# A gated DeltaNet stage: decay rows loaded a pair ahead, convolutions without cleared columns, block merges ordered behind a value's transposes

## The chip, the cores and the metric

One core of a Trainium2 chip runs the whole program in one launch. The metric is the device time of that launch in microseconds (us), the median of several runs. Three runs of the kernel before took 2161.83, 2160.51 and 2162.01 us, median 2161.83.

The core has TensorE (PE; its weight loads are PEld), VectorE (DVE), ScalarE (ACT), GpSimd (POOL) and SyncE (SP). Here every DMA is issued from SP, in one queue and in order. Each engine works through its own list in order as well: an instruction that waits holds up all that stand behind it on that engine.

## The reference, cut to what matters

Two layers of a decoder on 512 prompt tokens and 8 sample tokens, model width 1024: a gated DeltaNet mixer, an MLP, a dilated sliding-window attention, an MLP. The change touches the DeltaNet alone:

```python
proj = x @ w_in                                  # q | k | v | z | b | a
qkv, new_buf = causal_conv_silu(qkv, conv_buf, conv_w)   # 4 taps along time, zeros before the prompt's start
q, k = l2norm(q) * dk ** -0.5, l2norm(k)         # 8 heads, shared by 16 value heads
beta, g = sigmoid(b), -exp(a_log) * softplus(a + dt_bias)
gc = cumsum(g)                                   # within a chunk
decay = where(causal, exp(gc[i] - gc[j]), 0)
a_strict = where(strict, (beta * k) @ k.T * decay, 0)
t_inv = inverse(eye + a_strict)                  # unit lower triangular
u, w = t_inv @ (beta * v), t_inv @ (beta * k * exp(gc))
# a scan over chunks with state S (128 x 128 per head):
v_new = u - w @ S
o = (q * exp(gc)) @ S + (q @ k.T * decay) @ v_new
S = S * exp(gc_last) + (k * exp(gc_last - gc)).T @ v_new
y = (rmsnorm(o) * silu(z)) @ w_out
```

The outputs also hold the last three rows before the convolution (prompt_state_conv, sample_state_conv).

## The kernel before, in words

All four stages keep x transposed on chip, model width on the partitions and 520 tokens (512 prompt, 8 sample) in the free dimension. A product with a weight (`Common.proj`, L156) runs as three float32r passes (L164 to L166: high by high, high by low, low by high) over 8 blocks of 128 rows, in two halves of 260 columns: 48 matmuls for 128 output features. Weights come from memory by SP (L145), ACT rounds them to a high part (L130) and DVE subtracts for the low part (L131).

The DeltaNet stage (`gdn`, L367) goes over 8 pairs of value heads; a pair shares a q/k head, and a chunk is 128 tokens, so a pair has 4 chunks by 2 heads = 8 units. Of a pair p:

- `key` and `query` (L542, L561) and `values` (L681) project 128 features each through `project` (L509). It clears 3 columns of a row tile `pre` on POOL (L512), copies the projection behind them (L516, L518, on ACT), copies the 8 sample columns to `news` (L519) and the prompt's last three columns to `tail` (L522, on POOL), and runs the four taps: one on ACT (L524), three on DVE (L526), which read `pre` at shifts 2, 1, 0; then tanh into a third row tile (L528) and the product with it (L530). Eight row tiles go round.
- `decay` (L584) loads gc of each token, as a row, to all 128 partitions (L591, 512 KB, from the DRAM tile `Dg`), straight into the tile `ET` (two buffers). DVE subtracts the column (L592), ACT takes the absolute value and exp (L593, L594), and DVE multiplies with the dot products of the keys (L607) to `E` (L599).
- `invert` (L618) sends the 32 x 32 diagonal blocks of E through DRAM (L625, L628) to POOL, which inverts them by 62 multiply and add instructions in a row (L634, L637), and sends them back (L638, L642) into `Uf`, a part of `held`.
- `attend` (L610) turns ET into the masked attention (L614, L615).
- `merge` (L645) builds the 128 x 128 inverses from the 32 x 32 blocks: three DVE transposes (L649 to L651) and small matmuls (L656, L664, L667, L673, L678) with ACT copies between.
- `values` also transposes its two convolved rows on PE (L690) into PSUM and scales them on DVE (L691).
- `scan` (L694) runs the four chunks: L705, L708, L711, L713, L716, L720, L727, L731. The last reader of ET is L727 of the last chunk.
- `sample` (L792) updates the sample's states: matmuls (L812), small DVE operations (L813 to L819), a transpose on PE (L822), a sum on PE (L838). `out` (L843) normalises and gates (L855, L858, transposes L863 on PE, L865 on DVE); `out_proj` multiplies with the output weights (L888 adds to x).

What sets the order: the program is written in the order of L898 to L932, and a planner at build time orders each engine's list, by its own estimate of when operands are ready and by priority. `decay`, `invert`, `merge`, `scan`, `sample` and `out` are `urgent` (L33): priority 2000 places ahead of their place in the text, so before projections that are written far above them. Tiles of one tag are handed out in the order of the text; the PSUM tag `pre` has two banks, for L577, L607, L690 and L863 alike, so the bank of pair p's L690 comes free when DVE has read L863 of pair p-1 (L865). Merge of pair 0 (L903) stands ahead of the loop, that of a later pair at L915.

Of the kernel before, what the change touches and what calls it, by code (L numbers as in the profile page):

```python
# [10 lines left out]
F32 = mybir.dt.float32  # L11
# [8 lines left out]
P = 128  # L20
# [346 lines left out]
def gdn(K, l, done):  # L367
# [8 lines left out]
    with ExitStack() as ctx:  # L376
# [6 lines left out]
        sizes = dict(Uf0=U * P, Uf1=U * P, T64=U * 64, hist=32 * 3 * NS, news=32 * NS, eyeU=8 * 32, convw=32 * CONV, tri=P, Uo0=8 * 32, Uo1=8 * 32, tail=32 * 3, beg=160, gcl=128, egc=192, sbc=256, id8=8, onorm=1, alog=16, dtb=16, bat=160)  # L383
# [3 lines left out]
        Ufs, T64, hist, news = [part("Uf0", P), part("Uf1", P)], part("T64", 64)[:64], part("hist", 3 * NS), part("news", NS)  # L387
        eyeU, convw, tri, tail = part("eyeU", 32), part("convw", CONV), part("tri", P)[:, 0], part("tail", 3)
# [117 lines left out]
        def row(name):  # L506
            return K.tile(gp, [P, T], F32, tag="row", name=name, bufs=8)

        def project(w, ft, dest=None):  # L509

            pre = row("pre")
            nc.gpsimd.memset(pre[:, 0:3], 0.0)  # L512

            def ev(ps, hf, s):
                if hf == 0:
                    nc.scalar.copy(pre[:, 3 : 3 + H], ps)  # L516
                else:
                    nc.scalar.copy(pre[:, 3 + H : 3 + NP], ps[:, : H - NS])  # L518
                    nc.scalar.copy(news[:, ft, :], ps[:, H - NS :])  # L519

            K.proj(w, mov, ev)
            nc.gpsimd.tensor_copy(tail[:, ft, :], pre[:, NP : NP + 3])  # L522
            a = row("conv")[:, :NP]
            nc.scalar.activation(a, pre[:, 3 : 3 + NP], AF.Copy, scale=convw[:, ft, 3:4])  # L524
            for j in (2, 1, 0):
                nc.vector.scalar_tensor_tensor(a, pre[:, j : j + NP], convw[:, ft, j : j + 1], a, ALU.mult, ALU.add)  # L526
            t = row("tanh")[:, :NP]
            nc.scalar.activation(t, a, AF.Tanh)  # L528
            dest = a if dest is None else dest
            nc.vector.scalar_tensor_tensor(dest, t, 1.0, a, ALU.add, ALU.mult)  # L530
            return dest

        class Pair:
# [48 lines left out]

            @urgent
            def decay(self):  # L584


                p, hh, kq, col = self.p, self.hh, self.kq, self.col
                E = self.E = K.tile(gp, [P, U, P], F32, tag="E", name="E", bufs=2)
                ET = self.ET = K.tile(gp, [P, U, P], F32, tag="ET", name="ET", bufs=2)
                E4 = ET.rearrange("p (c v) d -> p c v d", v=2)  # L590
                nc.sync.dma_start(E4, Dg[None, :, hh, :].to_broadcast([P, C4, 2, P]))  # L591
                nc.vector.tensor_tensor(E4, E4, gc[:, :, hh, None].to_broadcast([P, C4, 2, P]), ALU.subtract)  # L592
                nc.scalar.activation(ET, ET, AF.Abs)  # L593
# [164 lines left out]
            def sample_conv(self, i0, n, f0):  # L758
# [4 lines left out]
                nc.vector.tensor_tensor(a[:, d], news[:, fs], wj(3), ALU.mult)  # L763
# [140 lines left out]
        for p in range(QK_HEADS):  # L904
# [29 lines left out]
        nc.sync.dma_start(O["sample_state_conv"][l, :, 0:2, :], sc[:, 1:3, :])  # L934
        for i in range(2):
            ps = K.bank("cb")
            nc.tensor.transpose(ps[:, :P], news[:, 16 * i : 16 * i + 16, :].rearrange("p f b -> p (f b)"), ident)
# [5 lines left out]
        nc.tensor.transpose(ps[:96, :P], tail.rearrange("p f j -> p (f j)"), ident)  # L943
# [448 lines left out]
```

## Time and profile before

| what | us |
|---|---|
| median of three runs | 2161.83 |
| the profiled execution, its own time | 2166.66 |
| its span, first to last instruction | 2164.9 |
| PE busy in the span | 1992.7 (92%) |
| DVE busy | 1312.6 (61%) |
| ACT busy | 893.7 (41%) |
| POOL busy | 519.7 (24%) |

The profiled execution is 4.83 us above the median, and 1.8 us of its time lie outside the span. The DeltaNet stage takes about the first 790 us; the first MLP follows to about 1215 us, then the attention and the second MLP. Busy PE is an upper bound of its work, since matmuls overlap; the granted clock says at how much of 2.4 GHz TensorE ran.

### The profile page before, as it was taken

What the parts mean: (1) busy time and instruction counts of PE and PEld (TensorE: products, weight loads), DVE (VectorE), ACT (ScalarE), POOL (GpSimd) and SP (SyncE); (2) the same over time, 40 slices, a digit from 0 to 9 for tenths busy, and PEclk for the clock granted to TensorE, in tenths of its full rate; (3) what the DMA queues carried; (4) which work ended last, traced back from release to release, by engine and by line L of the source; (5) the groups of instructions that cost most, each with busy time, mean ns of one, the idle gap of its engine ahead of it and who ended that gap; (6) DMA issues with size and microseconds to landing.
All of it is one profiled execution on the core that took longest, in us unless ns stands there. A gap on an engine that the chain in (4) does not pass through costs nothing.

```text
span 2164.9 us, 41794 instructions
## 1 busy us (share of the span) xinstructions
PE 1992.7 (92%) x16436; PEld 1958.9 (90%) x16436; DVE 1312.6 (61%) x3299; ACT 893.7 (41%) x2391; POOL 519.7 (24%) x813
## 2 busy tenths in 40 slices
PE   8768887977987989999999999999999989999998
PEld 7768877977877879999999999999999989999998
DVE  4745866757675585454455557676766785544444
ACT  4434444444344353323244545555555434233231
POOL 1262254535244230000001123332332250000000
PEclk8879889999889789999999999999999999999999
DMA  5324454765654538676766775544445342333332
GB/s 141 82 57 132 148 156 126 216 177 166 188 159 136 176 112 301 232 249 228 252 228 207 245 226 131 140 114 116 130 123 145 98 112 79 91 96 89 97 89 79
DMA packets 416278, 328.56 MB, mean 152 GB/s; under 512 B 48408, under 2 KB 404568, under 8 KB 413896
## 3 DMA queue, kind: packets, MB, share of 16 engines
q1 hardware_dynamic: 416080, 325.88, 50.0%
q8 instruction: 129, 2.11, 0.4%
q14 instruction: 69, 0.57, 0.1%
HBM read 302.19 MB, written 132.83 MB: 201 GB/s over the span
## 4 chain that ended last, share of the span: by engine, by line
PE 63%; DMA 11%; DVE 10%; POOL 9%; issue 4%; ACT 3%; SPq 1%; POOLq 0%; DVEq 0%; ACTq 0%
PE mm L164 18%; PE mm L166 18%; PE mm L165 18%; DMA Ft<-D 4%; POOL held L637 3%; POOL fs L634 3%; DMA ET<-Dg 2%; DMA X<-base 1%; DVE wlo L131 1%; DMA D<-held 1%; PE po L1199 1%; PE tr L1052 1%; DVE conv L526 1%; PE sco L1119 1%; DMA base<-X 1%
## 5 line engine op out<-in xcount | busy, mean ns | idle before, releaser
L164 PE MATMUL mm<-split,whi 128*128 128x260 f32 (+1 forms) x2960 | 866.9, 293 | 3.5 <-DVE base L781 2.3
L166 PE MATMUL mm<-split,wlo 128*128 128x260 f32 (+1 forms) x2960 | 854.7, 289 | 7.9 <-DVE wlo L131 7.9
L165 PE MATMUL mm<-split,whi 128*128 128x260 f32 (+1 forms) x2960 | 850.2, 287 | 0.5 <-DVE split L178 0.5
L166 PEld LDWEIGHTS mm<-split,wlo 128*128 128x128 f32 (+1 forms) x2960 | 567.5, 192 | 10.2 <-DVE wlo L131 9.2
L164 PEld LDWEIGHTS mm<-split,whi 128*128 128x128 f32 (+1 forms) x2960 | 568.6, 192 | 6.8 <-issue 2.7
L165 PEld LDWEIGHTS mm<-split,whi 128*128 128x128 f32 (+1 forms) x2960 | 568.2, 192 | 1.4 <-DVE split L178 0.7
L130 ACT CAST whi<-raw 128x1024 fp32r<-128x1024 f32 (+1 forms) x273 | 285.5, 1046 | 436.4 <-PE mm L165 414.8
L131 DVE TENSOR_TENSOR wlo<-raw,whi 128x1024 fp32r<-128x1024 f32 (+1 forms) x273 | 339.6, 1244 | 195.7 <-ACT whi L130 186.4
L166 PE MATMUL mm<-hh,wlo 128*128 128x260 f32 x1024 | 288.7, 282 | 0.0
L165 PE MATMUL mm<-hl,whi 128*128 128x260 f32 x1024 | 288.6, 282 | 0.0
L164 PE MATMUL mm<-hh,whi 128*128 128x260 f32 x1024 | 288.3, 283 | 0.0
L165 PEld LDWEIGHTS mm<-hl,whi 128*128 128x128 f32 x1024 | 193.1, 189 | 0.0
L166 PEld LDWEIGHTS mm<-hh,wlo 128*128 128x128 f32 x1024 | 192.8, 188 | 0.0
L164 PEld LDWEIGHTS mm<-hh,whi 128*128 128x128 f32 x1024 | 192.2, 188 | 0.0
L346 DVE TENSOR_TENSOR t<-mm,bc 128x260 f32<-128x260 f32 x128 | 54.8, 428 | 152.9 <-PE mm L166 152.9
L190 POOL TENSOR_TENSOR acc<-acc,sq 128x260 f32<-128x260 f32 x42 | 37.6, 906 | 386.3 <-ACT sq L189 385.9
L634 POOL TENSOR_TENSOR fs<-Ft,held 128x60 f32<-128x60 f32 (+24 forms) x248 | 93.0, 375 | 95.0 <-DMA Ft<-D 77.2
L130 ACT CAST hh<-q 128x260 fp32r<-128x260 f32 x128 | 52.4, 410 | 121.1 <-DVE q L333 121.1
L637 POOL TENSOR_TENSOR held<-held,fs 128x60 f32<-128x60 f32 (+24 forms) x248 | 95.6, 386 | 18.7
L526 DVE SCALAR_TENSOR_TENSOR conv<-pre,held,conv 128x512 f32<-128x512 f32 x96 | 78.7, 820 | 29.4 <-POOL pre L512 29.0
L164 PE MATMUL mm<-onh,whi 128*128 128x260 f32 x256 | 88.7, 350 | 7.2 <-DVE base L888 6.1
L131 DVE TENSOR_TENSOR hl<-q,hh 128x260 fp32r<-128x260 f32 x128 | 54.8, 428 | 57.0 <-ACT hh L130 57.0
(379 smaller groups left out, 3270.3 us busy)
## 6 DMA issues: line engine op xcount, KB each, us to landing
out_dram<-in_cache_kv_w_dram SPq DMA_DIRECT2D x112, 832.0 KB
raw<-in_dsw_w_in_dram SPq DMA_DIRECT2D x72, 512.0 KB
raw<-in_mlp_w_up_dram SPq DMA_DIRECT2D x64, 512.0 KB
raw<-in_mlp_w_down_dram SPq DMA_DIRECT2D x64, 512.0 KB
raw<-in_gdn_w_in_dram SPq DMA_DIRECT2D x48, 512.0 KB
S<-in_state_gdn_dram SPq DMA_DIRECT2D x16, 512.0 KB
raw<-in_gdn_w_out_dram SPq DMA_DIRECT2D x16, 512.0 KB
ub<-Du SPq DMA_DIRECT2D x16, 512.0 KB
```

What stands on the lines that cost most here:

```text
L130: nc.scalar.copy(hi, src)
L131: nc.vector.tensor_tensor(lo, src, hi.bitcast(F32), ALU.subtract)
L164: nc.tensor.matmul(ps[:m], lhsT=w[0][:, k, :m], rhs=xh[:, s], start=k == 0, stop=False)
L165: nc.tensor.matmul(ps[:m], lhsT=w[0][:, k, :m], rhs=xl[:, s], start=False, stop=False)
L166: nc.tensor.matmul(ps[:m], lhsT=w[1][:, k, :m], rhs=xh[:, s], start=False, stop=k == nk - 1)
L190: nc.gpsimd.tensor_tensor(acc[:, s], acc[:, s], t, ALU.add)
L346: nc.vector.tensor_tensor(t, ps, r2[:, s], ALU.mult)
L526: nc.vector.scalar_tensor_tensor(a, pre[:, j : j + NP], convw[:, ft, j : j + 1], a, ALU.mult, ALU.add)
L634: nc.gpsimd.tensor_tensor(tmp[:, :m, :n], Ft[:, None, j + 1 :, j].to_broadcast([P, m, n]), Uo[:, :m, j : j + 1].to_broadcast([P, m, n]), A ...
L637: nc.gpsimd.tensor_tensor(Uo[:, :m, j + 1 :], Uo[:, :m, j + 1 :], tmp[:, :m, :n], ALU.add)
L1052: nc.tensor.transpose(pst[:, c], f[:, c * P : (c + 1) * P], ident)
L1119: nc.tensor.matmul(o, lhsT=qf[:, c * P : (c + 1) * P], rhs=kf[:, k0 * P : (c + 1) * P], start=True, stop=True)
```

## The change

Three parts, all in `gdn`:

1. `load_rows` is split from `decay`. It loads the rows of gc into a tile `rows` of its own (one buffer). Pair 0's rows are loaded ahead of its key, pair 1's behind pair 0's `decay`, and pair p+2's, with priority 2000, right behind `decay` of pair p+1. `decay` reads `rows` and writes ET.
2. `project` no longer clears columns. `pre` starts at column 0; tap j covers only the columns for which it has an input (511, 510 and 509 columns). Both halves are copied by one line; the last 11 columns (3 of the prompt, 8 of the sample) go to `news` in one copy, and the copy to `tail` on POOL is gone. Tanh goes into `pre`, so a projection needs two row tiles instead of three. At the end of the stage two DVE copies split `news` into two flat tiles, which the last transposes read.
3. `merge` of pairs 1 to 7 is traced under `issue_after` of two instructions: its DVE instructions are queued behind L530 of the pair's first value, and its PE instructions behind the last of the four L690 transposes of that value. This is an order of issue on the engine, with no semaphore of its own.

```diff
-sizes = dict(... news=32 * NS, ... tail=32 * 3, ...)
+sizes = dict(... news=32 * (3 + NS), ...)
 def project(w, ft, dest=None):
     pre = row("pre")
-    nc.gpsimd.memset(pre[:, 0:3], 0.0)
     def ev(ps, hf, s):
-        if hf == 0:
-            nc.scalar.copy(pre[:, 3 : 3 + H], ps)
-        else:
-            nc.scalar.copy(pre[:, 3 + H : 3 + NP], ps[:, : H - NS])
-            nc.scalar.copy(news[:, ft, :], ps[:, H - NS :])
+        nc.scalar.copy(pre[:, s], ps)
+        if hf:
+            nc.scalar.copy(news[:, ft], ps[:, H - NS - 3 :])
     K.proj(w, mov, ev)
-    nc.gpsimd.tensor_copy(tail[:, ft, :], pre[:, NP : NP + 3])
     a = row("conv")[:, :NP]
-    nc.scalar.activation(a, pre[:, 3 : 3 + NP], AF.Copy, scale=convw[:, ft, 3:4])
+    nc.scalar.activation(a, pre[:, :NP], AF.Copy, scale=convw[:, ft, 3:4])
     for j in (2, 1, 0):
-        nc.vector.scalar_tensor_tensor(a, pre[:, j : j + NP], convw[:, ft, j : j + 1], a, ALU.mult, ALU.add)
-    t = row("tanh")[:, :NP]
+        n = NP - 3 + j
+        nc.vector.scalar_tensor_tensor(a[:, NP - n :], pre[:, :n], convw[:, ft, j : j + 1], a[:, NP - n :], ALU.mult, ALU.add)
+    t = pre[:, :NP]
     nc.scalar.activation(t, a, AF.Tanh)
     dest = a if dest is None else dest
-    nc.vector.scalar_tensor_tensor(dest, t, 1.0, a, ALU.add, ALU.mult)
+    convs[0] = nc.vector.scalar_tensor_tensor(dest, t, 1.0, a, ALU.add, ALU.mult).ins
+def load_rows(self):
+    self.rows = K.tile(gp, [P, C4, 2, P], F32, tag="rows", name="rows", bufs=1)
+    nc.sync.dma_start(self.rows, Dg[None, :, self.hh, :].to_broadcast([P, C4, 2, P]))
 def decay(self):
-    nc.sync.dma_start(E4, Dg[None, :, hh, :].to_broadcast([P, C4, 2, P]))
-    nc.vector.tensor_tensor(E4, E4, gc[:, :, hh, None].to_broadcast([P, C4, 2, P]), ALU.subtract)
+    rows = self.rows
+    nc.vector.tensor_tensor(E4, rows, gc[:, :, hh, None].to_broadcast([P, C4, 2, P]), ALU.subtract)
 def values(self):
     for v in range(2):
         vf = project(wv[v], self.fts[2 + v])
+        if v == 0:
+            self.conv0 = convs[0]
...
         for c in range(C4):
-            nc.tensor.transpose(pst[:, c], vf[:, c * P : (c + 1) * P], ident)
+            flip = nc.tensor.transpose(pst[:, c], vf[:, c * P : (c + 1) * P], ident)
+        if v == 0:
+            self.flip0 = flip.ins
+pairs[0].load_rows()
 pairs[0].key()
 pairs[0].decay()
+pairs[1].load_rows()
...
     if p < last:
         pairs[p + 1].key()
         pairs[p + 1].decay()
+        if p + 1 < last:
+            with tc.high_priority(2000):
+                pairs[p + 2].load_rows()
...
     if p:
-        A.merge()
+        with tc.issue_after(A.conv0), tc.issue_after(A.flip0):
+            A.merge()
...
+flat = K.tile(gp, [P, 32 * (3 + NS)], F32, tag="flat", name="flat", bufs=1)
+tail, fresh = flat[:, : 32 * 3], flat[:, 32 * 3 :]
+nc.vector.tensor_copy(tail.rearrange("p (f j) -> p f j", j=3), news[:, :, :3])
+nc.vector.tensor_copy(fresh.rearrange("p (f b) -> p f b", b=NS), news[:, :, 3:])
```

## Rows read from the trace of the kernel before

**Rows 1.** The profile's page: the chain that ended last, its shares by engine.
```profile
PE 63%; DMA 11%; DVE 10%; POOL 9%; issue 4%; ACT 3%; SPq 1%; POOLq 0%; DVEq 0%; ACTq 0%
```

**Rows 2.** Stretches: engines' busy time (instructions), granted clock, DMA share, GB/s.
```profile
core 0: us, PE busy (x) PEld busy (x) DVE busy (x) ACT busy (x) POOL busy (x), PEclk, DMA share, GB/s
200.00:400.00 200.00, 169.70 (x1454) 163.18 (x1453) 135.98 (x417) 89.08 (x270) 77.57 (x155) 0.89 0.53 155
...
800.00:1200.00 400.00, 400.00 (x3321) 399.23 (x3321) 200.61 (x368) 138.99 (x276) 14.04 (x24) 1.00 0.70 240
```

**Rows 3.** Waits of PE, 0 to 800 us: waited for, us in total, times, longest.
```profile
PE sut L822 <- DVE base L815: 35.4, 6, 11.1
PE px L656 <- DMA held<-D: 16.2, 3, 6.0
PE son L838 <- DVE base L836: 9.1, 1, 9.1
PE sst L778 <- DVE base L766: 7.5, 1, 7.5
```

**Rows 4.** Waits of DVE, 0 to 800 us.
```profile
DVE held L649 <- DMA held<-D: 50.0, 6, 21.1
DVE ET L592 <- DMA ET<-Dg: 43.8, 8, 7.9
DVE conv L526 <- POOL pre L512: 29.0, 9, 6.6
```

**Rows 5.** Timelines of SP, DVE and PE at pair 2's rows: start, length, engine, line.
```profile
207.76 0.37 SPq L591 DMA_DIRECT2D ET<-Dg  x1
...
217.84 1.23 DVE L592 TENSOR_TENSOR ET<-ET,held 128x1024 f32<-128x1024 f32 x1 [7.43 <-DMA ET<-Dg]
...
219.59 0.28 PE L822 MATMUL sut<-base 128*16 128x128 f32 x1 [4.01 <-DVE base L815]
```

**Rows 6.** Timelines of DVE and PE where the same wait meets a merge.
```profile
451.30 0.43 DVE L649 STREAM_TRANSPOSE held<-held 32x256 f32<-32x256 f32 x1 [5.92 <-DMA held<-D]
...
451.92 0.37 PE L822 MATMUL sut<-base 128*16 128x128 f32 x1 [11.14 <-DVE base L815]
```

**Rows 7.** Stretches of PE before and behind that wait (columns as above).
```profile
437.80:440.80 3.00, 2.98 (x24) 2.77 (x24) 0.00 (x0) 0.27 (x1) 2.33 (x11) 1.00 0.80 84
452.00:455.50 3.50, 3.50 (x18) 3.50 (x17) 2.78 (x10) 0.26 (x1) 0.00 (x0) 0.50 1.22 405
```

**Rows 8.** Timeline of DVE at the second of the first two decays.
```profile
83.36 1.23 DVE L592 TENSOR_TENSOR ET<-ET,held 128x1024 f32<-128x1024 f32 x1 [3.42 <-DMA ET<-Dg]
```

**Rows 9.** Timelines of DVE and PE: a convolution's tap and the scan behind it.
```profile
592.86 0.88 DVE L526 SCALAR_TENSOR_TENSOR conv<-pre,held,conv 128x512 f32<-128x512 f32 x1 [6.56 <-POOL pre L512]
...
594.49 1.22 PE L705 MATMUL pk<-S,kq 128*128 128x256 f32 x2 [4.32 <-DVE S L720]
```

**Rows 10.** Timelines of PE and DVE: merge and first transposes of pairs 1, 2, 7.
```profile
224.82 0.56 PE L656 MATMUL px<-held,E 32*32 32x32 f32 x12
...
236.12 0.69 PE L690 MATMUL vtr<-base,conv 128*128 128x128 f32 x2
...
302.54 1.72 PE L656 MATMUL px<-held,E 32*32 32x32 f32 x32 [5.75 <-DMA held<-D]
...
305.78 0.74 DVE L865 SCALAR_TENSOR_TENSOR ot<-otr,held,sz 128x512 f32<-128x512 f32 x1
...
310.10 0.44 PE L690 MATMUL vtr<-base,conv 128*128 128x128 f32 x2
...
707.97 0.42 PE L656 MATMUL px<-held,E 32*32 32x32 f32 x4
...
724.40 0.38 PE L690 MATMUL vtr<-base,conv 128*128 128x128 f32 x2
```

**Rows 11.** Stretches of two POOL inversions, pair 1's and pair 2's (columns as above).
```profile
141.00:176.20 35.20, 34.82 (x331) 34.02 (x332) 26.27 (x74) 16.39 (x39) 30.89 (x69) 0.89 0.23 71
267.80:294.70 26.90, 23.24 (x184) 23.00 (x183) 11.67 (x39) 13.24 (x36) 22.15 (x61) 0.94 0.38 123
```

More of the change, by code (lines that the diff above doesn't have):

```diff
@@ L380, in gdn @@
         gp = setup.enter_context(tc.tile_pool(name="gset", bufs=1))
-        sizes = dict(Uf0=U * P, Uf1=U * P, T64=U * 64, hist=32 * 3 * NS, news=32 * NS, eyeU=8 * 32, convw=32 * CONV, tri=P, Uo0=8 * 32, Uo1=8 * 32, tail=32 * 3, beg=160, gcl=128, egc=192, sbc=256, id8=8, onorm=1, alog=16, dtb=16, bat=160)
+        sizes = dict(Uf0=U * P, Uf1=U * P, T64=U * 64, hist=32 * 3 * NS, news=32 * (3 + NS), eyeU=8 * 32, convw=32 * CONV, tri=P, Uo0=8 * 32, Uo1=8 * 32, beg=160, gcl=128, egc=192, sbc=256, id8=8, onorm=1, alog=16, dtb=16, bat=160)
         held = cp.tile([P, sum(sizes.values())], F32, name="held")
@@ L386, in gdn @@
         part = lambda n, d: held[:, at[n] : at[n] + sizes[n]].rearrange("p (a d) -> p a d", d=d)
-        Ufs, T64, hist, news = [part("Uf0", P), part("Uf1", P)], part("T64", 64)[:64], part("hist", 3 * NS), part("news", NS)
-        eyeU, convw, tri, tail = part("eyeU", 32), part("convw", CONV), part("tri", P)[:, 0], part("tail", 3)
+        Ufs, T64, hist, news = [part("Uf0", P), part("Uf1", P)], part("T64", 64)[:64], part("hist", 3 * NS), part("news", 3 + NS)
+        eyeU, convw, tri = part("eyeU", 32), part("convw", CONV), part("tri", P)[:, 0]
         beg = part("beg", 16).rearrange("p (c t) h -> p c t h", t=2)
@@ L507, in row @@
             return K.tile(gp, [P, T], F32, tag="row", name=name, bufs=8)
+        convs = [None]
         def project(w, ft, dest=None):
             pre = row("pre")
-            nc.gpsimd.memset(pre[:, 0:3], 0.0)
             def ev(ps, hf, s):
-                if hf == 0:
-                    nc.scalar.copy(pre[:, 3 : 3 + H], ps)
-                else:
-                    nc.scalar.copy(pre[:, 3 + H : 3 + NP], ps[:, : H - NS])
-                    nc.scalar.copy(news[:, ft, :], ps[:, H - NS :])
+                nc.scalar.copy(pre[:, s], ps)
+                if hf:
+                    nc.scalar.copy(news[:, ft], ps[:, H - NS - 3 :])
             K.proj(w, mov, ev)
-            nc.gpsimd.tensor_copy(tail[:, ft, :], pre[:, NP : NP + 3])
             a = row("conv")[:, :NP]
-            nc.scalar.activation(a, pre[:, 3 : 3 + NP], AF.Copy, scale=convw[:, ft, 3:4])
+            nc.scalar.activation(a, pre[:, :NP], AF.Copy, scale=convw[:, ft, 3:4])
             for j in (2, 1, 0):
-                nc.vector.scalar_tensor_tensor(a, pre[:, j : j + NP], convw[:, ft, j : j + 1], a, ALU.mult, ALU.add)
-            t = row("tanh")[:, :NP]
+                n = NP - 3 + j
+                nc.vector.scalar_tensor_tensor(a[:, NP - n :], pre[:, :n], convw[:, ft, j : j + 1], a[:, NP - n :], ALU.mult, ALU.add)
+            t = pre[:, :NP]
             nc.scalar.activation(t, a, AF.Tanh)
             dest = a if dest is None else dest
-            nc.vector.scalar_tensor_tensor(dest, t, 1.0, a, ALU.add, ALU.mult)
+            convs[0] = nc.vector.scalar_tensor_tensor(dest, t, 1.0, a, ALU.add, ALU.mult).ins
             return dest
@@ L762, in sample_conv @@
                 wj = lambda j: convw[:, fs, j : j + 1].to_broadcast([P, n, NS])
-                nc.vector.tensor_tensor(a[:, d], news[:, fs], wj(3), ALU.mult)
+                nc.vector.tensor_tensor(a[:, d], news[:, fs, 3:], wj(3), ALU.mult)
                 for j in range(3):
@@ L934, in gdn @@
         nc.sync.dma_start(O["sample_state_conv"][l, :, 0:2, :], sc[:, 1:3, :])
+        flat = K.tile(gp, [P, 32 * (3 + NS)], F32, tag="flat", name="flat", bufs=1)
+        tail, fresh = flat[:, : 32 * 3], flat[:, 32 * 3 :]
+        nc.vector.tensor_copy(tail.rearrange("p (f j) -> p f j", j=3), news[:, :, :3])
+        nc.vector.tensor_copy(fresh.rearrange("p (f b) -> p f b", b=NS), news[:, :, 3:])
         for i in range(2):
             ps = K.bank("cb")
-            nc.tensor.transpose(ps[:, :P], news[:, 16 * i : 16 * i + 16, :].rearrange("p f b -> p (f b)"), ident)
+            nc.tensor.transpose(ps[:, :P], fresh[:, P * i : P * (i + 1)], ident)
             r = K.tile(gp, [P, P], F32, tag="junk", name="cb", bufs=2)
@@ L942, in gdn @@
         ps = K.bank("cb")
-        nc.tensor.transpose(ps[:96, :P], tail.rearrange("p f j -> p (f j)"), ident)
+        nc.tensor.transpose(ps[:96, :P], tail, ident)
         r = K.tile(gp, [P, P], F32, tag="junk", name="cbt", bufs=2)
```

## The prediction

> **What bounds the kernel now.** I read the chain that ended last first: PE has 63% of it, DMA, DVE and POOL 30% together [rows 1]. The stretches say where those 30% sit. From 800 us on PE is never idle and its granted clock is 1.00; from 200 to 400 us, inside the DeltaNet stage, it is busy 169.70 of 200 us at 0.89 [rows 2]. So the rest of the kernel is bound by TensorE and the change does not touch it; the stage of the change, some 790 us long, is bound by what PE waits for. The table of PE's waits names it [rows 3], and that of DVE says why [rows 4]. 35.4 us go to L822, the transpose of the sample's update, which waits for a tiny DVE operation (L815). That operation is late because DVE stands still: in 43.8 us it waits at L592 for decay's rows, in 50.0 at the first of merge's transposes (L649), in 29.0 at a convolution's tap for a cleared column. DVE is an in-order list, so one wait for a DMA becomes everybody's.
>
> One case in full [rows 5]: SP issues pair 2's rows at 207.76, as soon as the scan two pairs back has released the ET buffer; L592 starts at 217.84, 10.1 us later, and DVE was idle for 7.43 of them; only then come L813 to L815, and PE, which had run out of other work in its list, starts L822 at 219.59 after 4.01 us idle.
>
> **Part 1, the rows a pair ahead.** A separate tile takes the load out of the release of ET. The same eight loads of 512 KB are issued, one each, so DMA traffic is unchanged. On SP's list a load now waits for L592 of the pair before instead of L727, and is issued about a pair earlier; the engines' mean DMA share there is 0.53 [rows 2], so it has room, and a landing late by several us is covered by the rest of the pair. L592 still waits for ET's release by L727, which is an engine's wait and no DMA's. The 43.8 us of DVE are the upper bound for DVE; what counts is PE's 35.4 in six waits. Of these some have a second cause: in the one of 11.14 us DVE stood at L649 from 445.4 to 451.30, 5.92 us, with L815 behind it [rows 6]. That is merge's wait and stays. I let 9 us stay in all (this 5.92, and half as much again for another of the kind) and take 26; the bounds are 17 and 35.4.
>
> At the start it may cost. Today the first two loads fly together and the second L592 runs at 83.36 after 3.42 us of waiting [rows 8]. With one buffer of rows, pair 1's load is issued only behind pair 0's L592, at about 79.9 (83.36 less 3.42); with the 10.1 us above it lands at 90.0, 6.6 later than now. If that L592 stays ahead of pair 0's E in DVE's list, the first inversion is 6.6 later and nothing covers it; if E goes first, the 7.5 us of L778 [rows 3] go as well. Bounds: a loss of 6.6, a gain of 7.5; I take a loss of 2, nearer to the row of the second L592.
>
> **Part 2, no cleared columns.** 32 clears and 32 small copies leave POOL; what they cost is not their length but their place, behind POOL's chain of 62 inversion steps. DVE's taps waited 29.0 us in nine cases [rows 4]. In the longest, 6.56 us, the scan's state update stood behind the tap and PE lost 4.32 at L705 [rows 9]: two thirds. Two thirds of all would be 19; zero is the other bound, for a tap that holds up nobody. I take 12, since only some of the nine fall into a scan. The shortened taps and the wider copies to `pre` and `news` keep their shapes to within a few columns: no difference. Two row tiles per projection instead of three let projections run further ahead; they already do, so nothing. The two added DVE copies at the stage's end have 96 and 256 columns and are shorter than L592's 1.23 us with 1,024 [rows 5]: 0.6 us, bounds 0 and 2.5, with out_proj of the last pair as cover.
>
> **Part 3, merge behind the first value's transposes.** DVE's half of the order changes nothing: the convolution it names is done long before. PE's half does. PE waits 16.2 us at L656 for the inverted blocks in three pairs [rows 3]; if four transposes and other matmuls go ahead of it, at most 16.2 is gained. Against it: L690 needs a PSUM bank that DVE frees by L865, after the pair before has been transposed out. In pair 2 L656 starts at 302.54 and L865 ends at 306.52, because it stands behind merge's own L649 on DVE; so PE may wait at L690 instead, and merge comes 4 us later [rows 10]. Behind the delayed merge stand the scan, then ET's release. How far merge could slip is read from how far the transposes follow it now: 11.3, 7.6 and 16.4 us in pairs 1, 2 and 7 [rows 10], mean 11.8, over seven pairs 82. I take 10 gained at L656 and 12 lost by later scans, a loss of 2: most of the slip should be absorbed, because the sample and output chain of the pair before, which now goes first, no longer shares PE and DVE with merge. Bounds: a gain of 16, a loss of 41 (half of 82).
>
> **The clock.** Ahead of the 11.14 us wait 24 matmuls take 3.0 us at granted clock 1.00 (2.4 GHz); behind it 18 take 3.5 at 0.50 (1.2 GHz) [rows 7]. At the first rate those 18 would take 2.25, so a long idle stretch costs 1.25 us more after it ends. Some five such stretches fewer give 6; bounds 0 and 10.
>
> **Sum.** 26 - 2 + 12 - 0.6 - 2 + 6 = 39.4 us. The profiled execution took 2166.66, 4.83 above the median of 2161.83; 2166.66 - 39.4 - 4.83 = 2122.4. I predict 2122.
>
> **The rivals.**
>
> *Merge comes too late* (slower). The place is the PSUM tag `pre`: merge of pair p now stands in line behind out of pair p-1, where today both run side by side, and the scan follows in series. The price is the 82 us above. Everything else gains 41.4; if half of the 82 reaches the end the change is worth nothing, if two thirds do (55), the kernel takes 2161.8 + 13.6 = 2175. For it: the distances, and that the last scan has little work of others beside it. Against: PE has projections to fill with. Chance 0.12.
>
> *The inversion's chain takes it all back.* E, the trip to POOL, 62 steps and the trip back are one chain per pair; if it is the true bound, what L822 gives up reappears at L656. POOL's steps depend on how busy DVE is: pair 1's inversion took 35.2 us with DVE busy 26.27 (75%), pair 2's 26.9 with DVE busy 11.67 (43%) [rows 11]. That is 8.3 us for 31 points. A DVE that no longer waits is busier during inversions: 10 points more would be 2.7 us each, 21 in eight pairs. Then the 26 of part 1 are gone and 3 of the clock's 6: 10.4 us remain, 2151. Against it: DVE's total work is the same, so what is done sooner is missing later. Chance 0.22.
>
> The Trainium skill, GPSIMD Engine Reference, Specifications, says that GpSimd shares its SBUF interfaces with VectorE and that DVE instructions with two SBUF inputs contend with it. By that rule L592, the taps and the low parts of weights, all with two such inputs, would slow the inversion; the two rows agree with it in sign.
>
> *More goes than I counted.* All upper bounds together (35.4 + 7.5 + 19 + 16 + 10 = 88) would give 2074; halfway from my sum, 2098. For it: a period that shrinks lets the next release come earlier as well. Against: L649's 50.0 us on DVE stay. Chance 0.16.
>
> *No effect*: the planner orders every list anew, and DVE's next wait, L649, takes the place of L592. 2162, chance 0.06.
>
> My forecast has 0.44; its own range is 2108 to 2140.
>
> **How the numbers follow.** Forecast, chain and more-than-counted are all faster: 0.44 + 0.22 + 0.16 = 0.82. Within 0.2% (4.3 us, about what a measurement of this kernel can tell from no change) 0.06, slower 0.12. The range reaches from 2088, which leaves out the lower third of the third rival, to 2160, which takes in the chain's 2151 and leaves out the slower case and no effect.
>
> **What would show it.** Right: the wait of DVE at L592 falls from 43.8 to under 8; L822's from 35.4 to about 9; no wait of L526 for POOL; the stretch 200 to 400 busier than 169.70 and its clock above 0.89. Part 3 right: L656 below 16.2 without a new wait of the same size at L690 or L711. Wrong: PE idle at L656 or L690 by as much as L822 lost; merges starting 8 us or more later against the pair's E; inversions of 30 us and over; the first E later than now by 5 us or more.

## The result, and the profile after

The changed kernel takes 2149.88 us (median of 4 runs, 2149.18 to 2152.49), the kernel before beside it 2161.92: a ratio of 0.9933, interval 0.9910 to 0.9957. That is 12 us, where 39.4 were forecast. The profiled execution took 2152.49 us, with a span of 2150.7 against 2164.9, so the traces hold 14.2 us of difference. (Here and below the ratios and intervals are the recorded ones; they differ a little from quotients of the medians, which would give 0.9944 here.)

The page's first part, span and busy time:

```profile
span 2150.7 us, 41729 instructions
PE 1972.8 (92%) x16436; PEld 1937.4 (90%) x16436; DVE 1319.7 (61%) x3301; ACT 892.5 (41%) x2391; POOL 500.4 (23%) x749
```

Read this first, against 1992.7 us of PE in 2164.9 before: the same 16,436 matmuls take 19.9 us less, and PE's idle time, span less busy, goes **up**, from 172.2 to 177.9. Whatever the change won, it did not win it by letting PE wait less. Line numbers have moved: L592 is now L596, L649 to L651 are L653 to L655, L656 is L660, L690 is L696, L822 is L830, L863 is L871.

The stretches, columns as in [rows 2]:

```profile
core 0: us, PE busy (x) PEld busy (x) DVE busy (x) ACT busy (x) POOL busy (x), PEclk, DMA share, GB/s
0.00:200.00 200.00, 160.20 (x1300) 155.36 (x1301) 114.99 (x335) 82.34 (x206) 68.21 (x161) 0.88 0.44 111
200.00:400.00 200.00, 159.77 (x1409) 153.17 (x1408) 138.59 (x409) 86.19 (x266) 74.26 (x141) 0.87 0.55 149
400.00:600.00 200.00, 173.71 (x1516) 168.53 (x1516) 152.62 (x442) 91.28 (x271) 86.51 (x175) 0.94 0.63 187
600.00:800.00 200.00, 156.18 (x1256) 147.75 (x1256) 124.53 (x349) 79.68 (x226) 67.74 (x115) 0.84 0.47 144
800.00:1200.00 400.00, 400.00 (x3323) 399.60 (x3323) 201.08 (x368) 139.58 (x288) 14.03 (x24) 1.00 0.70 242
```

From 200 to 400 us PE is busy less than in [rows 2] (159.77 against 169.70) and at a lower clock. From 800 to 1200 us nothing has changed. Now the waits of PE and of DVE up to 830 us:

```profile
PE px L660 <- DMA held<-D: 24.8, 1, 24.8
PE otr L871 <- DVE osb L866: 22.6, 3, 12.4
PE sut L830 <- DVE base L823: 18.0, 1, 18.0
PE mm L164 <- DVE base L848: 17.4, 1, 17.4
PE mm L166 <- DVE wlo L131: 13.1, 4, 11.4
PE son L846 <- DVE base L844: 11.6, 1, 11.6
PE mm L164 <- DVE ET L618: 6.3, 2, 4.1
```

```profile
DVE held L653 <- DMA held<-D: 91.0, 7, 19.6
...
DVE held L654 <- DMA held<-D: 26.7, 1, 26.7
...
DVE ET L596 <- DMA rows<-Dg: 7.8, 2, 4.1
```

The waits that the change aims at are gone: L596 for rows 7.8 us (43.8 in [rows 4], and both that remain lie at the start), no tap waits for POOL (29.0). But the first of merge's transposes wait 117.7 us (91.0 + 26.7), where before they waited 65.7 (50.0, and 15.7 at L650):

```profile
DVE held L650 <- DMA held<-D: 15.7, 3, 9.1
```

DVE got 65 us back and stands 52 us longer at its next DMA. PE has fewer and longer waits: one for 18.0 us at L830 instead of six for 35.4 [rows 3]. For pair 0's blocks it waits 24.8 us at L660; before it was

```profile
PE px L656 <- POOL fs L634: 15.7, 1, 15.7
```

One of the longer waits of the changed kernel, DVE and then PE:

```profile
268.45 0.22 DVE L844 TENSOR_TENSOR base<-base 128x16 f32<-128x16 f32 x1
288.24 0.43 DVE L653 STREAM_TRANSPOSE held<-held 32x256 f32<-32x256 f32 x1 [19.57 <-DMA held<-D]
...
289.67 0.17 DVE L848 TENSOR_SCALAR base<-son 128x16 f32<-128x16 f32 x1
```

```profile
272.16 0.30 PE L786 MATMUL sst<-base 128*128 128x24 f32 x2
289.90 0.59 PE L164 MATMUL mm<-split,whi 128*128 128x260 f32 x1 [17.44 <-DVE base L848]
290.28 0.42 PE L165 MATMUL mm<-split,whi 128*128 128x260 f32 x1
290.50 0.42 PE L166 MATMUL mm<-split,wlo 128*128 128x260 f32 x1
...
293.19 0.29 PE L164 MATMUL mm<-split,whi 128*128 128x260 f32 x1
293.31 0.28 PE L165 MATMUL mm<-split,whi 128*128 128x260 f32 x1
```

Two stretches of PE behind that wait, columns as in [rows 2]:

```profile
290.00:292.80 2.80, 2.80 (x13) 2.80 (x14) 2.63 (x12) 0.00 (x0) 0.00 (x0) 0.50 0.14 21
293.20:296.20 3.00, 3.00 (x28) 3.00 (x27) 2.60 (x6) 1.85 (x4) 0.00 (x0) 1.00 1.01 367
```

DVE stands 19.57 us at merge's transpose, with L848, 0.17 us long, behind it; PE needs it and idles 17.44. Then 14 projection matmuls run at a granted clock of 0.50 (1.2 GHz), one every 0.22 us (290.28, 290.50), before the clock is 1.00 (2.4 GHz) and the rate one in 0.12 (293.19, 293.31). So a stretch of idle time costs its length and a piece behind it. The matmuls of L164 to L166 that stood over 0.34 us in the records before the stage's last L871 number 512 of 3,036 before, 329 of 3,032 after: 183 fewer, at 0.10 us each (0.22 less 0.12) some 18 us. That is nearly all of the 19.9 that PE's busy time lost.

The wait shown is not the only one of its kind. In each of pairs 2 to 7 DVE stands once at L653 (19.6, 10.0, 13.9, 14.1, 18.5 and 11.2 us), and with each stand PE waits too, for a DVE operation queued behind it (17.4, 8.9, 11.6, 11.4, 18.0 and 12.4 us): what was several waits of a pair now comes in one piece.

### The profile page after: what moved, and what is told of

Same layout as the page of the kernel before. It is cut to its first block, busy times and chain, and to the rows that moved or that the text cites. A ratio compares the mean times of both kernels' runs of the same rounds, so it can differ in the third digit from the quotient of the medians.

```text
span 2150.7 us, 41729 instructions
## 1 busy us (share of the span) xinstructions
PE 1972.8 (92%) x16436; PEld 1937.4 (90%) x16436; DVE 1319.7 (61%) x3301; ACT 892.5 (41%) x2391; POOL 500.4 (23%) x749
## 5 line engine op out<-in xcount | busy, mean ns | idle before, releaser
L164 PE MATMUL mm<-split,whi 128*128 128x260 f32 (+1 forms) x2960 | 861.7, 291 | 22.0 <-DVE base L848 17.4
L166 PE MATMUL mm<-split,wlo 128*128 128x260 f32 (+1 forms) x2960 | 849.1, 287 | 20.3 <-DVE wlo L131 20.3
L164 PEld LDWEIGHTS mm<-split,whi 128*128 128x128 f32 (+1 forms) x2960 | 564.2, 191 | 24.5 <-DVE base L848 17.5
L166 PEld LDWEIGHTS mm<-split,wlo 128*128 128x128 f32 (+1 forms) x2960 | 563.1, 190 | 23.3 <-DVE wlo L131 22.5
L166 PE MATMUL mm<-hh,wlo 128*128 128x260 f32 x1024 | 289.1, 283 | 0.0
L164 PE MATMUL mm<-hh,whi 128*128 128x260 f32 x1024 | 287.9, 282 | 0.0
L166 PEld LDWEIGHTS mm<-hh,wlo 128*128 128x128 f32 x1024 | 192.6, 188 | 0.0
L164 PEld LDWEIGHTS mm<-hh,whi 128*128 128x128 f32 x1024 | 192.3, 188 | 0.0
L638 POOL TENSOR_TENSOR fs<-Ft,held 128x60 f32<-128x60 f32 (+24 forms) x248 | 90.3, 364 | 112.1 <-DMA Ft<-D 93.4
L641 POOL TENSOR_TENSOR held<-held,fs 128x60 f32<-128x60 f32 (+24 forms) x248 | 90.4, 364 | 19.4
L164 PE MATMUL mm<-onh,whi 128*128 128x260 f32 x256 | 85.2, 336 | 2.8 <-DVE ET L618 2.2
L839 POOL TENSOR_TENSOR ub<-ub,base 128x1024 f32<-128x1024 f32 x16 | 32.7, 2044 | 216.7 <-DMA ub<-Du 201.6
```

Source lines behind the costliest of these rows:

```text
L164: nc.tensor.matmul(ps[:m], lhsT=w[0][:, k, :m], rhs=xh[:, s], start=k == 0, stop=False)
L166: nc.tensor.matmul(ps[:m], lhsT=w[1][:, k, :m], rhs=xh[:, s], start=False, stop=k == nk - 1)
L638: nc.gpsimd.tensor_tensor(tmp[:, :m, :n], Ft[:, None, j + 1 :, j].to_broadcast([P, m, n]), Uo[:, :m, j : j + 1].to_broadcast([P, m, n]), A ...
L641: nc.gpsimd.tensor_tensor(Uo[:, :m, j + 1 :], Uo[:, :m, j + 1 :], tmp[:, :m, :n], ALU.add)
L839: nc.gpsimd.tensor_tensor(ub, ub, kqs[:, :, 0:1].to_broadcast([P, NS, P]), ALU.mult)
```

## The experiments

**Runs 1 to 4: parts alone.** First theory: the stage is one loop through merge's transposes, so a wait taken from DVE is waited there. Run 1, part 1 alone:

```diff
-                nc.sync.dma_start(E4, Dg[None, :, hh, :].to_broadcast([P, C4, 2, P]))
-                nc.vector.tensor_tensor(E4, E4, gc[...
+                rows = self.rows
+                nc.vector.tensor_tensor(E4, rows, gc[...
```

> Part 1 alone on the kernel before. Theory (a loop sets the pace: a pair's inverted blocks land, DVE's list lets merge's first transpose go ahead of the output step of the pair before, whose PSUM banks gate the next pair's E, and from E to the blocks it is some 50 us): DVE's wait at the decay rows falls from 43.8 to under 10 us, its wait at merge's first transposes rises from 65.7 to 90 or more, and the time moves by less than 10 us, 2152 to 2165. Rival (the waits removed are worth what I forecast, and the order of part 3 gives it back): 2130 to 2140.

Measured 2173.28 us, ratio 1.0059 (1.0032 to 1.0085): slower. The wait for decay's rows is gone but for the start, and merge's first two transposes wait 90.9 us, as the theory has it, but the time lies above its 2152 to 2165, and PE's idle time rises to 181.2 (span 2171.8 less 1990.6), which it does not explain.

Run 2, part 2 alone:

```diff
-            nc.gpsimd.memset(pre[:, 0:3], 0.0)
...
-                nc.vector.scalar_tensor_tensor(a, pre[:, j : j + NP], convw[:, ft, j : j + 1], a, ALU.mult, ALU.add)
+                n = NP - 3 + j
+                nc.vector.scalar_tensor_tensor(a[:, NP - n :], pre[:, :n], convw[:, ft, j : j + 1], a[:, NP - n :], ALU.mult, ALU.add)
```

> Part 2 alone. Theory (the loop): no DVE wait for POOL's clear any more (29.0 before), merge's transposes wait longer than 65.7, the time moves by less than 10 us, 2152 to 2165. Rival (removed waits are worth what I forecast): about 2150, 12 us below before.

Measured 2158.19, ratio 0.9976 (0.9964 to 0.9989). The tap waits are gone, merge's transposes wait 84.5, and the time is within the theory's 2152 to 2165.

Run 3, part 3 alone:

```diff
-                A.merge()
+                with tc.issue_after(A.conv0), tc.issue_after(A.flip0):
+                    A.merge()
```

> Part 3 alone. Theory (the loop): merge's matmuls come 7 to 19 us behind the blocks, but the loop runs through DVE's transposes and not through them, so the time moves by less than 8 us, 2154 to 2170. Rival (part 3 gives back what parts 1 and 2 gain): 2175 to 2190.

Measured 2160.44, ratio 0.9992 (0.9975 to 1.0009), within the theory's range. PE's wait for blocks remains in pair 0 only (14.8), and 21.5 us appear at otr behind DVE.

Run 4, parts 1 and 2, without the two lines of part 3:

```diff
-                with tc.issue_after(A.conv0), tc.issue_after(A.flip0):
-                    A.merge()
+                A.merge()
```

> The changed kernel without part 3: parts 1 and 2. Theory (the loop): within 8 us of the changed kernel, 2142 to 2158, with DVE's wait at merge's transposes near 100 us. Rival (part 3 gives back the gain): 2120 to 2130.

Measured 2164.13, ratio 1.0006 (0.9986 to 1.0026), above the theory's 2142 to 2158. Its waits of PE, then of DVE:

```profile
PE px L660 <- DMA held<-D: 63.2, 4, 24.6
PE sut L830 <- DVE base L823: 21.9, 1, 21.9
PE sst L786 <- DVE base L784: 18.9, 1, 18.9
PE son L846 <- DVE base L844: 18.6, 1, 18.6
```

```profile
DVE held L653 <- DMA held<-D: 77.4, 7, 21.9
DVE held L654 <- DMA held<-D: 43.5, 2, 26.4
```

Of both parts' DVE waits (43.8 and 29.0 us) 9.0 are left, all at the start; 55 reappear at the blocks (120.9 less 65.7), and PE now waits for them too. Part 3 added to this kernel makes the changed one, and it goes the way opposite to a cost.

**Runs 5 and 6: the loop.** If DVE's stand at L653 holds up the loop, merge belongs behind the output chain of the pair before.

```diff
-                        nc.vector.scalar_tensor_tensor(t, ps[:, : n * P], onorm, szs[:, v, s], ALU.mult, ALU.mult)
+                        self.gated = nc.vector.scalar_tensor_tensor(t, ps[:, : n * P], onorm, szs[:, v, s], ALU.mult, ALU.mult).ins
...
-                with tc.issue_after(A.conv0), tc.issue_after(A.flip0):
+                with tc.issue_after(A.conv0), tc.issue_after(A.flip0), tc.issue_after(pairs[p - 1].gated):
```

> The changed kernel, but merge's instructions of a pair also stand behind the last gated output (L873) of the pair before, so that VectorE no longer waits for the inverted blocks with the rest of the output chain queued behind it. Theory of the loop (blocks, merge's transposes at the head of VectorE's list, output chain of the pair before, the shared PSUM bank, the next E, the next inversion): in the changed kernel VectorE's wait at L653 delays otr (L871) by 9 to 12 us in the pairs where TensorE waits longest there; each E then comes about that much earlier, TensorE's waits at otr fall from 22.6 to under 6 us, VectorE's waits at L653 and L654 from 117.7 to under 70, and the kernel takes 2100 to 2130. Rival, the inversion's chain by itself (E, transfer, 62 steps, transfer): the blocks land no earlier, the same time is waited somewhere else, and the kernel takes 2145 to 2155. Rival, the lists: merge now comes too late for its own scan, and the kernel takes 2160 or more.

Measured 2166.64, ratio 1.0014 (0.9993 to 1.0036). DVE's waits at the blocks fall from 117.7 to 34.1 us (24.8 of them pair 0's), but pair 4's E comes at 418.5 us instead of 399.7, and the time is that of the second rival. Run 6 keeps the new condition alone:

```diff
-                with tc.issue_after(A.conv0), tc.issue_after(A.flip0):
+                with tc.issue_after(pairs[p - 1].gated):
```

> The changed kernel with merge's instructions only behind the last gated output (L873) of the pair before, and no longer behind the first value's convolution and transposes. Theory of the loop: VectorE's order is what counts, so this is within 5 us of the kernel with all three conditions, 2100 to 2135. Rival, that the change's own order (behind the first value) is what gives its 0.7% on top of the other two parts: without it the time is near 2164, as with parts 1 and 2 alone.

Measured 2172.50, ratio 1.0027 (1.0011 to 1.0043); the first of its waits of PE:

```profile
PE px L660 <- DMA held<-D: 101.2, 7, 24.3
```

The wait left DVE and went to PE, and the time lies far above the theory's 2100 to 2135 and above the rival's 2164 as well. The loop through DVE's list falls: the head of that list is one place where the wait can be, not its cause.

**Runs 7 and 8: the inversion shortened**, in the changed kernel and in the one before.

```diff
-                for j in range(31):
+                for j in range(24):
```

> The changed kernel with 24 instead of 31 steps of the inversion; the last seven steps of each 32x32 block are left out. In pair 3's inversion those seven take 5.5 of 26.9 us on GpSimd (359.9 to 365.4 us). Theory of the loop: every pair's blocks land about 5.5 us earlier, VectorE's waits at L653 and L654 lose most of that, and seven passes of the loop give 25 to 38 us: 2112 to 2125. Rival, that the loop isn't closed by the inversion (TensorE's idle time comes from the order of the lists): under 10 us, 2140 to 2150, and the wait at L653 shrinks without the E's coming earlier.

> The kernel before with 24 instead of 31 steps of the inversion, the last seven steps of each 32x32 block left out. Theory of the loop: the kernel before is bound by the same loop, so it gains nearly as much as the changed kernel, 20 to 38 us: 2125 to 2142. Rival, that before is bound by the decay rows and the cleared columns and only the changed kernel by the inversion: here under 10 us, 2152 to 2162, while the changed kernel gains 25 or more.

Measured 2159.62 (0.9981, 0.9964 to 0.9998) and 2186.93 (1.0081, 1.0050 to 1.0112). Pair 4's blocks reach DVE at 443.1 us instead of 450.8, yet neither kernel is faster than with all 31 steps, and in run 7 the waits at L653 and L654 do not shrink (118.0 us, 117.7 in the changed kernel). Shortening every pair's chain by some 5 us bought nothing, which speaks against the chain of inversions as the bound of the stage: the 20 to 38 us of the theory are missing, and a gain of a few us could be hidden by what runs 11 to 16 show. That both became slower fits no theory so far, and both times lie outside all the ranges named: an edit that removes work cost up to 0.8%. What it also does is reorder the lists: compared line by line, by operation and operands, PE's matmuls of runs 7 and 8 differ in 655 and 1,641 lines from those of the same kernel with 31 steps.

**Runs 9 and 10: the other pairs of parts** (1 with 3, then 2 with 3; the hunks are those above).

> Parts 1 and 3 without part 2. Theory of the lists (TensorE's span is 1943 us, plus its idle time, plus 0.108 us for each projection of the stage that runs at half clock; an edit reorders every engine's list, and how the idle time falls out is not the sum of the waits it removes): VectorE's waits at merge's transposes rise above 85 us, the span agrees with that sum within 4 us, and the time lies anywhere from 2145 to 2180, not at the product of the two parts alone. Rival, that the parts act by themselves: 1.0059 times 0.9992 of 2164, 2175 to 2178. Rival, that part 3 is what lets part 1 pay: 2150 to 2157.

> Parts 2 and 3 without part 1. Theory of the lists: span equals 1943 plus idle plus 0.108 us for each half-clock projection within 4 us; the time lies anywhere from 2145 to 2180. Rival, that the parts act by themselves: 0.9976 times 0.9992 of 2164, 2155 to 2159. Rival, that part 3 is what lets part 2 pay: 2148 to 2154.

Measured 2172.85 (1.0023, 1.0006 to 1.0041) and 2166.56 (1.0005, 0.9989 to 1.0022): neither the product of the single effects nor the rival's gain. In run 9 merge's transposes wait 106.9 us, as expected, but its span is some 6 us under the sum of 1943 us, idle time (here only that ahead of PE's last matmul, 5 to 6 us less than span less busy) and half-clock projections; run 10's is within 2. Over the two kernels compared and runs 1 to 16 that sum holds within about 3 us for ten and misses by 5 to 13 for eight, so I use PE's busy time from here.

**Runs 11 to 16: arrangements.** Three edits that neither add nor remove anything, each on the kernel before and on the changed one: the four small transfers of an inversion's blocks reversed (runs 11, 12), merge's two small products swapped (13, 14), the scan's two residuals swapped (15, 16).

```diff
-                for b in range(4):
+                for b in (3, 2, 1, 0):
...
-                for o in (0, 64):
+                for o in (64, 0):
...
-                        for v in range(2):
+                        for v in (1, 0):
```

> The kernel before, with the four small transfers of an inversion's blocks issued in the reverse order; not a byte or an operation more or less. The lists of TensorE and VectorE come out in another order all the same. Theory of the lists: the time moves by 4 to 15 us in either direction, with the idle time and the half-clock projections that account for it. Rival, that a reordering alone is worth nothing and only removed work or waits are: 2161 to 2167, within 0.15% of the kernel before.

> The changed kernel with the same reversal of the four small transfers. Its lists differ from those of the changed kernel in far fewer places than those of the kernel before do. Theory of the lists: 2 to 10 us from the 2150 of the changed kernel, in either direction. Rival, that a reordering alone is worth nothing: 2148 to 2152.

> The kernel before, with merge's two small block products taken in the order 64, 0 instead of 0, 64: the same operations, another order of the lists. Theory of the lists alone (an arrangement draws its time from a spread of about 0.8% either way, and the change is worth nothing beyond that): between 2148 and 2185, not systematically above the kernel before. Rival, that the change removes a real 0.5% or more and the arrangement adds a spread around it: kernels with the change stay below those without it, so this one lies above 2152 and above its counterpart with the change by 10 us or more.

> The changed kernel with the same swap, 64 before 0. Theory of the lists alone: between 2148 and 2185, and not nearer to 2150 than to 2164. Rival, that the change removes a real 0.5% or more: below 2155, and 10 us or more below its counterpart without the change.

> The kernel before, with the scan's two residuals of a chunk (L708) computed in the order 1, 0: the same operations, another order of the lists. Theory of the lists alone: between 2148 and 2185, not systematically above its counterpart with the change. Rival, that the change removes a real 0.5% or more: above 2152 and 10 us or more above its counterpart.

> The changed kernel with the same swap of the two residuals; its lists differ from the changed kernel's in fewer places (some 950 lines of TensorE's list against 2800 in the kernel before). Theory of the lists alone: within 10 us of the changed kernel in either direction, as a list that differs little. Rival, that the change removes a real 0.5% or more: 2140 to 2155, and 10 us or more below its counterpart without the change.

Times in us, ratios to the kernel before on the same chip; busy and idle time of PE (span less busy) are from the page:

| kernel | time | ratio (interval) | busy | idle |
|---|---|---|---|---|
| before, as it is | 2161.92 | 1 | 1992.7 | 172.2 |
| 11, before, reversed | 2185.11 | 1.0077 (1.0052 to 1.0103) | 2015.4 | 171.5 |
| 13, before, products | 2191.58 | 1.0129 (1.0112 to 1.0146) | 2014.1 | 177.5 |
| 15, before, residuals | 2179.27 | 1.0061 (1.0041 to 1.0081) | 1991.8 | 177.4 |
| changed, as it is | 2149.88 | 0.9933 (0.9910 to 0.9957) | 1972.8 | 177.9 |
| 12, changed, reversed | 2146.60 | 0.9903 (0.9879 to 0.9926) | 1963.7 | 177.3 |
| 14, changed, products | 2145.42 | 0.9912 (0.9898 to 0.9927) | 1970.8 | 174.1 |
| 16, changed, residuals | 2155.21 | 0.9958 (0.9945 to 0.9972) | 1970.1 | 181.4 |

The busy lines of runs 11 and 12:

```profile
PE 2015.4 (92%) x16436; PEld 1977.2 (90%) x16436; DVE 1321.5 (60%) x3299; ACT 890.6 (41%) x2391; POOL 519.8 (24%) x813
```

```profile
PE 1963.7 (92%) x16436; PEld 1929.6 (90%) x16436; DVE 1313.9 (61%) x3301; ACT 892.3 (42%) x2391; POOL 499.8 (23%) x749
```

The rival of runs 11 and 12, that a reordering is worth nothing, falls: run 11 is 20 us above the kernel before beside it (2165.13), more than the 4 to 15 expected. In runs 13 to 16 the rival, a real 0.5% or more, is borne out: the counterparts are 46 and 24 us apart (run 16, at 2155.21, is a hair above that rival's range), while runs 13 and 14 lie outside the theory's 2148 to 2185.

This answers the main question. An arrangement alone moves the kernel before by up to 1.3%, twice what the change did; so a single ratio says little of a mechanism. But the two sets do not overlap: mean ratios 1.0067 and 0.9927, 0.0140 apart or 30 us, with a standard error of 0.003 from the spread within each four. That error is on the small side, since the changed four are nearer to one another: in the same line by line comparison runs 12 and 16 differ from the changed kernel in 215 and 285 lines and run 14 in 1,313, where runs 11, 13 and 15 differ from the kernel before in 1,249 to 1,693. And all of the difference is busy time (of one profiled execution of each): the means are 2003.5 and 1969.4 (34 less), idle time 174.7 and 177.7 (3 more). The kernel before is the lowest of its own four; against its three neighbours (mean 1.0089) it is some 19 us better than they are. If they stand for its arrangements, the change gave that up and gained more.

PE's idle stretches of over 1 us between 60 us and the stage's end, counted in the traces of the four kernels before: 27, 34, 25, 32, in sum 126.5 us on average; of the four changed ones 17, 22, 20, 17, in sum 130.0. The same idle time comes in a third fewer pieces, and the half-clock projections behind them fall from 512, 601, 592, 522 to 329, 328, 368, 351. The granted clock says the same. Up to the stage's last L871 it falls to 0.50 in 22, 26, 23 and 25 spells before and in 15, 11, 14 and 13 after. PE is busy in these spells for 160.6 us on average before and 89.9 after, 6.7 and 6.8 us in each. Of the 71 us that are gone, work at the full rate saves 0.10 of every 0.22, so some 32 us of the 34: an estimate from the two rates above. It is not the count alone: run 4's 13 spells hold 118.5 us.

**Runs 17 and 18: which part.** The first two neutral edits on the kernel of run 4.

```diff
-                for b in range(4):
+                for b in (3, 2, 1, 0):
```

> Parts 1 and 2 without part 3, with the four small transfers of the blocks in the reverse order (a second arrangement of the kernel that took 2164). Theory, that part 3 has a worth of its own: TensorE waits 50 us or more for inverted blocks at L660, its idle time stays near 180 us, and the time is 2157 to 2172, 10 us or more above the changed kernel with the same reversal (2146.6). Rival, that part 3 is worth nothing and the first arrangement of parts 1 and 2 was an unlucky one: 2140 to 2155.

```diff
-                for o in (0, 64):
+                for o in (64, 0):
```

> Parts 1 and 2 without part 3, with merge's two small block products in the order 64, 0 (a third arrangement). Theory, that part 3 has a worth of its own: as in the run before, 2157 to 2172, 10 us or more above the changed kernel with the same swap (2145.4), with TensorE's idle time near 180 us. Rival, that part 3 is worth nothing: 2140 to 2155.

Measured 2145.95 (0.9906, 0.9892 to 0.9919) and 2162.85 (0.9993, 0.9974 to 1.0012). Against the changed kernel in the same arrangement (0.9903, 0.9912, and 0.9933 beside run 4's 1.0006) part 3 is worth 0.0003, 0.0081 and 0.0073. One of three, run 17, sides with the rival; run 18 lies in the theory's range, with 70.0 us of waiting at L660 as expected. So part 3's own worth stays open between nothing and 0.8%. PE's busy time is steadier than the time, and tells more:

| parts | PE busy, each kernel | mean |
|---|---|---|
| none | 1992.7, 2015.4, 2014.1, 1991.8 | 2003.5 |
| one (1; 2; 3) | 1990.6; 1989.2; 1990.4 | 1990.1 |
| two (1+2 three times; 1+3; 2+3) | 1979.2, 1971.3, 1977.8; 1979.4; 1979.8 | 1977.5 |
| all | 1972.8, 1963.7, 1970.8, 1970.1 | 1969.4 |

From row to row the mean falls by 8 to 13 us. What each part takes by itself stays open: the three single kernels were run in one arrangement each and are only 2 to 4 us below the kernel before as it is. The idle time follows no such order: means of 174.7, 170.7, 185.6 and 177.7. Nor do the three parts make sure of the gain: run 5 holds them all and one more condition, and its PE is busy 1997.1 us.

## Why the prediction was wrong

**The step that failed** is the one on the waits: "I let 9 us stay in all ... and take 26" of PE's 35.4, and the 12 us of the taps beside it. Both subtract PE's idle time as if a wait that is removed were time that is gone. Measured, PE's idle time rose by 5.7 us in the profiled pair and by 3 over the four arrangements. The working had the warning in it: of the 11.14 us wait it left 5.92 because "DVE stood at L649" [rows 6]. That became the rule: with L592's and the taps' waits gone, DVE stands 52 us longer at merge's transposes, once in each of pairs 2 to 7, with operations that PE needs behind it, and PE idles 9 to 18 us with each stand.

**The clock** was the term that carries the change, and the one most undersized: 6 us with a bound of 10. The step counted 1.25 us for a long stretch of idle time and five stretches fewer [rows 7]. The direction was right: there are ten or so fewer (29.5 to 19 on average). But each of them costs more than the 1.25 us worked out from the 3.5 us of [rows 7]: PE's busy time fell by 19.9 us in the profiled pair, with ten stretches fewer, and by 34 over the arrangements. Summed over the matmuls of the stage in the traces, the projections gave 24 of these 34 (417 us before, 393 after, on average) and the scan's, the sample's and merge's own matmuls 8 (231 and 223).

**The arrangement** had no term at all. The text named it once, under "no effect" (the planner orders every list anew), as a way to lose the gain, and not as a spread of its own. It is larger than the bound of 0.2% that the chances used: three neutral edits moved the kernel before by 0.6 to 1.3%. With it, 39.4 us is not far from the 30 between the sets, but by way of a term that was wrong: the agreement is no merit of the sum.

By the other steps:

- *The start*, a loss of 2, bounds a loss of 6.6 and a gain of 7.5. The second L596 runs at 90.3, as worked out, and pair 0's E goes first (84.5 instead of 85.6), the case for which the gain was named; L778's 7.5 are gone. Yet pair 0's inversion starts at 108.3 instead of 102.1, and PE waits 24.8 us for its blocks where it waited 15.7. What the sum left out is in part 1 itself: in the twelve kernels that load the rows ahead pair 0's inversion starts 21.6 to 22.5 us after its last E, in the eight that do not 14.3 to 15.9. In the changed kernel's trace SP issues two loads of rows near it, at 81.7 us and, between the sending of the blocks (86.7) and their fetch (92.9), at 91.6; that the fetch waits behind these loads was not tried apart.
- *Part 3*, a loss of 2: PE no longer waits for blocks in any pair but 0, as forecast, and the only wait at L696 in the changed kernel is one of 1.0 us. In pairs 2 to 7 merge's first matmuls follow the blocks by 7 to 19 us. The wait is now at DVE's L653 and, behind it, at PE's L871, L830, L846 and two projections.
- *The added copies*: not visible, as costed.
- *The rest of the kernel*: "from 800 us on PE is never idle" holds for the row shown, up to 1200 us. From there to the end PE is idle for 29 us before and 28 after, so that the argument stands.

**The rivals.** *Merge too late* (2175): the sign that was named for it came, since in pairs 2 to 7 merge's matmuls start 66.0 us behind the pair's E on average, 55.5 before; the loss did not. The changed kernel is faster, and beside the same two parts without the order it is not slower in any of three arrangements. *The inversion's chain takes it all back* (2151) gave the nearest time by a mechanism that the runs do not bear out: inversions take some 25 to 28 us in pairs 2 to 7, not longer than before (26 to 29), and shortening them by 5 us each gained nothing in either kernel. Its sum also took off the 26 of part 1 where its own working gives 21. The sign "inversions of 30 us and over" came in pair 0 alone (31.0 us from the first step's start to the last one's end, 26.5 before), while pair 1's went from 35.5 to 29.3. What was right in it is the general form: the wait comes back at the next thing that is late. *More goes than counted* is refuted by the idle time. *No effect* named the right place, L649 in the place of L592, and missed what the fewer pieces give.

The price that rival drew from the share of DVE shows only faintly. Two of the inversions after, columns as in [rows 11]:

```profile
256.60:281.40 24.80, 15.86 (x135) 15.69 (x133) 6.08 (x19) 11.48 (x32) 20.04 (x61) 0.89 0.54 108
...
580.50:608.40 27.90, 20.92 (x168) 20.24 (x166) 17.06 (x48) 15.39 (x47) 23.15 (x61) 0.91 0.28 94
```

With DVE busy for 6.08 of 24.80 us (25%) the inversion takes 24.8, with 17.06 of 27.90 (61%) 27.9: 3.1 us for 36 points, where [rows 11] gave 8.3 for 31. Pair 0's took 31.0 us at 57% and 26.5 before at 55%, so the share does not set the time by itself. The Trainium skill, GPSIMD Engine Reference, Specifications, says that GpSimd shares its SBUF interfaces with VectorE; the trace agrees in sign, and leaves most of pair 1's 35.2 us unexplained.

## What to carry to other kernels

Where in-order engines wait for one another, a wait that is removed can move to the next late operand, as it did here; before it is booked as a gain, find the wait that comes next behind it, and book only what the bounding engine's idle **and** busy time would lose. Compare span less busy and busy by themselves: here nearly all of the gain was matmuls that ran at full clock, and idle time came in fewer pieces. And where a planner reorders everything after each edit, one pair of kernels can't tell a mechanism from an arrangement: make a neutral edit or two on both sides, and compare the sets. Here they also found the fastest versions: the changed kernel with the transfers reversed (0.9903) or merge's products swapped (0.9912), and run 17, without part 3 (0.9906), which their intervals do not tell apart.

## What the runs showed that I had not expected

- The order of four 32 x 32-block transfers, with no other change, moved the kernel before by 0.8% (0.5 to 1.0), and in the profiled executions all of that is PE's busy time (2015.4 against 1992.7, idle time 171.5 against 172.2).
- A long stretch of idle time costs little more behind it than one of medium length. In the stage of all twenty kernels' traces, 15.9 projections on average ran at half clock in the 12 us behind a stretch of 4 to 8 us, 17.0 behind one of 8 to 16 and 20.6 behind a longer one. The short ones are cheaper: 13.1 behind 2 to 4 us and 5.9 behind 1 to 2. Single cases scatter widely around these means.
- Removing seven of 31 steps from a chain of GpSimd work, some 5 us of about 27 in each pair, did not make the kernel faster, in either version.
